# Sums of the gated unit's products stored once in fp32 and split where they are used, with a new set of order constraints, in a two-layer encoder kernel

## The chip, the cores and the metric

The kernel runs on one core of a Trainium2 chip. The metric is the time of one execution on the device, in microseconds (us). The core has a matrix engine (PE, with its weight load PEld shown apart), a vector engine (DVE), a scalar engine (ACT), a general engine (POOL) and a queue engine (SP) that issues most of the DMA transfers. Each engine runs its own instructions in order.

## The reference, cut to what matters

The program is a two-layer trunk over 1024 frames of width 1024, in fp32, with batch 1. The part that the change touches is layer 0:

```python
proj = h @ w_in                      # h = rmsnorm(x); u_s5, g_s5, q, k, v, g_ret
y = gelu(s5(u_s5))                   # diagonal state-space layer
y = y * sigmoid(y @ glu_w + glu_b)   # the gated unit ("GLU")
y_s5 = y * silu(g_s5)
y_ret = retention(q, k, v) * silu(g_ret)     # 8 heads, normalised per head
x = x + concat([y_s5, y_ret]) @ w_out
```

Layer 1 is a convolution module (two pointwise products, a depthwise convolution of width 31, a layer norm, swish, a gate and an output product). A final norm ends the program.

## The kernel before

Activations are held transposed: 128 features on the partitions, time along the row, in two halves of 512 columns. Every fp32 product is made as three matmuls on numbers split into a high and a low part (`mm3`): high weight by high operand (L300), high weight by low operand (L301), low weight by high operand (L302). A matmul of 128x512 is the unit of the work of PE. For weights and operands alike ACT makes the high part (a cast, L278 for weights, L1489 for operands) and DVE or POOL subtracts it from the fp32 original to get the low part (L279 for weights, L1491 for operands).

The program runs in stages: input products and state-space layer (to about 316 us); keys, queries, values and retention, in four pairs of heads numbered 0 to 3 (to about 537 us); the products of the gated unit (`mm_glu...`, to about 610 us); the output product of layer 0 (`mm_wo`); and layer 1.

The product of the gated unit is done by a Strassen-like scheme: seven products of half size instead of eight, on sums of the four quarters of y and of the weights. `y_pass` makes the sums of y: for each of four row blocks (0 to 3) it loads two blocks of state-space output, applies gelu, stores the result to `yn_d` and forms the sums (`yn`, on POOL for the late passes, L1177 to L1180). For each of its two tiles it then casts to a high part `th` on ACT (L1184), stores that from ACT's queue (L1185), subtracts it on DVE (L1186, in place) and stores the low part from SP's queue (L1187). `glu_sums` does the like for the weights on POOL (`gs`, L1200 to L1203, stored to `ws_d`).

`layer0_back_and_layer1` runs the products. Its operands are `y11`, `y21`, `y22` (quarters, loaded in fp32 by `load_split` and split on the chip) and `yt1` to `yt4` (sums, loaded by `load_sum` as two ready halves, high and low, L1531). Product numbers are in the tile names: `mm_glu10` is product 1, `mm_glu60` product 6 and so on. `wf_glu0` to `wf_glu13` are its weight tiles as loaded, `wh_glu` and `wl_glu` the halves; each has three buffers. `gated` applies tanh, multiplies by `yg` and `yn` and splits the result to `ysh` and `ysl`.

Within a pair of retention, PE transposes the keys (`ktp`), DVE scales them (`kt`, L1388), PE makes states (`kv`) and scores (`sp`), DVE masks the scores (`sc`, L1428) and accumulates states (`S`), PE makes the outputs (`ro`), DVE takes their statistics (`st`, `mv`), ACT normalises (`on`, L1471, three buffers), PE transposes back (`rt`, L1479) and DVE multiplies by the gate (`grl`). Queries and keys are rotated before that by POOL (`krot`, `qrot`, L1282), after a transfer swaps their rows (`kswp`, `qswp`).

What sets the order: a scheduler orders each engine's instructions from a timeline of its own, and the table `ORDER` adds constraints. An entry (engine, late, early) says that on that engine the instruction named `late` is placed after the one named `early`; it sets places in a queue, and no engine waits for another by it. SP issues transfers strictly in its order, and an issue waits there until its source is written and its destination buffer is free.

Of the kernel before, what the change touches and what calls it, by code (L numbers as in the profile page):

```python
# [39 lines left out]
LANES = 2  # L40
ADDS = {"k": lambda nc: nc.gpsimd, "q": lambda nc: nc.gpsimd}
ORDER = (
    ('PE', ('turn', 0), ('mm_u6_0', 23)),
    ('PE', ('mm_u6_1', 0), ('turn', 3)),
    ('PE', ('v0_0', 0), ('mm_g8_0', 23)),
    ('PE', ('v1_0', 0), ('mm_g8_0', 23)),
    ('PE', ('kp_0', 0), ('mm_g8_0', 23)),
# [41 lines left out]
    ('PE', ('mm_wo0_0', 42), ('mm_wo1_0', 8)),  # L89
# [64 lines left out]
class Trunk:  # L154
# [995 lines left out]
    def y_pass(self, k, yp=None, tag="ynt"):  # L1150


        nc, v = self.nc, self.nc.vector
        held = yp is None
        pools = [self.rq, self.rq if held else yp]
        yns, yts = [], []
# [23 lines left out]
        eng.tensor_tensor(b21, b11, b21, op=ALU.subtract)  # L1180
        yield
        for i in range(2):
            hi = pools[i].tile([P, T], F32R, name=f"th{i}_{k}", tag="yp", bufs=1)
            nc.scalar.copy(hi[:], yns[i])  # L1184
            nc.scalar.dma_start(self.t_d[i, 0, k * P:(k + 1) * P], hi[:].bitcast(F32))  # L1185
            v.tensor_tensor(yns[i].bitcast(F32R), yns[i], hi[:].bitcast(F32), op=ALU.subtract)  # L1186
# [306 lines left out]
    def layer0_back_and_layer1(self, st):  # L1493
# [665 lines left out]
```

## Time and profile before

| | |
|---|---|
| Time, median of 3 runs | 1134.23 us (1133.91 to 1138.55) |
| Time of the profiled execution | 1135.55 us |
| Its span | 1133.7 us |
| Its mean granted clock of PE | 0.994 |
| PE busy | 1105.6 us (98%) |
| DVE busy | 812.3 us (72%) |
| ACT busy | 543.2 us (48%) |
| POOL busy | 657.0 us (58%) |
| Bytes moved by DMA | 279.47 MB, 247 GB/s on the mean |

The page gives busy time per engine, the span in slices, the DMA queues, the chain of work that ended last, and the costliest groups of instructions. A row of the timeline shows the start, the duration, the engine, the line and operation, out<-in, the shape, and in brackets the idle time of that engine just before, with what released it. A row of the waits shows which engine and line waited for which, the total in us, how often, and the longest. A row of the windows shows for one stretch the busy time of each engine, the granted clock of PE, the share of time in which the DMA engines were busy, and the rate.

### The profile page before, as it was taken

Reading aid. Unit: us, or ns where it says so; the run is one execution under the profiler, and the core shown is the slowest. Engines: PE = TensorE matmul, PEld = TensorE weight load, DVE = VectorE, ACT = ScalarE, POOL = GpSimd, SP = SyncE. Lnnn points to the kernel's source line nnn. Section 1 sums busy time; section 2 is a strip of 40 time slices with the busy share of each in tenths; the row PEclk is TensorE's granted clock in tenths of the full one; section 3 lists DMA queues with packets and bytes.
Section 4 is the critical chain, followed back from the end, with each engine's and each line's share of the span. In section 5 each row is a group of like instructions: output and inputs, shape, how many; then the busy total and the mean of one; then the engine's idle time right before and its main releaser. Section 6 shows DMA issues by size and latency. Waiting matters only on the chain.

```text
span 1133.7 us, 16979 instructions
## 1 busy us (share of the span) xinstructions
PE 1105.6 (98%) x6014; PEld 963.9 (85%) x6014; DVE 812.3 (72%) x1436; ACT 543.2 (48%) x835; POOL 657.0 (58%) x459
## 2 busy tenths in 40 slices
PE   9999999999999999996899999999999999999997
PEld 8888888888888888885778888888888888888886
DVE  6886866666525574578468632599999899999744
ACT  7313334443236541623546523555535677446773
POOL 3049957888455435564375011589544568779863
PEclk9999999999999999998999999999999999999999
DMA  8346767777897767879998998665778665356964
GB/s 318 112 138 172 220 195 239 252 264 263 299 319 240 249 220 260 267 243 289 389 361 290 345 321 272 208 231 198 242 255 291 242 198 177 121 185 233 329 237 176
DMA packets 136117, 279.47 MB, mean 247 GB/s; under 512 B 21089, under 2 KB 50017, under 8 KB 135905
## 3 DMA queue, kind: packets, MB, share of 16 engines
q1 hardware_dynamic: 129744, 257.16, 68.1%
q10 hardware_dynamic: 6288, 21.24, 4.8%
q8 instruction: 47, 0.77, 0.3%
q14 instruction: 38, 0.30, 0.1%
HBM read 191.65 MB, written 82.51 MB: 242 GB/s over the span
## 4 chain that ended last, share of the span: by engine, by line
PE 85%; DMA 5%; DVE 3%; ACT 2%; POOL 2%; issue 2%; SPq 0%; POOLq 0%; DVEq 0%; ACTq 0%
PE mm_g L300 7%; PE mm_g L302 7%; PE mm_g L301 7%; PE mm_v L1374 5%; PE mm_wo L302 5%; PE mm_wo L300 5%; PE mm_wo L301 5%; PE mm_b L301 2%; PE mm_b L302 2%; PE mm_a L301 2%; PE mm_b L300 2%; PE mm_a L302 2%; PE mm_a L300 2%; PE mm_u L301 2%; PE mm_u L300 2%; PE mm_u L302 2%
## 5 line engine op out<-in xcount | busy, mean ns | idle before, releaser
L1776 DVE SCALAR_TENSOR_TENSOR cv<-u,convw,cv 128x512 f32<-128x512 f32 x390 | 268.0, 752 | 5.9 <-ACT cv L1743 3.9
L1737 POOL TENSOR_TENSOR tp<-tp,tp 128x512 f32<-128x512 f32 x64 | 82.4, 1288 | 33.0 <-ACT tp L1736 32.1
L300 PE MATMUL mm_g<-xh,wh_g 128*128 128x512 f32 x256 | 97.8, 382 | 0.0
L301 PE MATMUL mm_g<-xl,wh_g 128*128 128x512 f32 x256 | 97.1, 379 | 0.0
L302 PE MATMUL mm_g<-xh,wl_g 128*128 128x512 f32 x256 | 96.0, 379 | 0.0
L567 POOL TENSOR_TENSOR s1q<-s1q,s1q 128x512 f32<-128x512 f32 x12 | 16.7, 1391 | 80.0 <-ACT s1q L562 71.3
L1736 ACT ACTIVATE tp<-u,convw 128x512 f32<-128x512 f32 x64 | 45.3, 718 | 33.4 <-POOL tp L1737 32.6
L300 PEld LDWEIGHTS mm_g<-xh,wh_g 128*128 128x128 f32 x256 | 48.5, 189 | 6.8 <-issue 0.2
L302 PEld LDWEIGHTS mm_g<-xh,wl_g 128*128 128x128 f32 x256 | 48.5, 189 | 6.8
L301 PEld LDWEIGHTS mm_g<-xl,wh_g 128*128 128x128 f32 x256 | 48.5, 189 | 6.6
L301 PE MATMUL mm_oc<-zl,wh_woc 128*128 128x512 f32 (+1 forms) x144 | 51.4, 357 | 0.2 <-DVE zl L1491 0.2
L300 PE MATMUL mm_oc<-zh,wh_woc 128*128 128x512 f32 (+1 forms) x144 | 51.1, 364 | 0.0
L302 PE MATMUL mm_oc<-zh,wl_woc 128*128 128x512 f32 (+1 forms) x144 | 50.8, 356 | 0.0
L300 PE MATMUL mm_g<-h1h,wh_cg 128*128 128x512 f32 x128 | 49.0, 383 | 0.0
L300 PE MATMUL mm_wo<-ysh,wh_wos 128*128 128x512 f32 x128 | 49.0, 382 | 0.0
L302 PE MATMUL mm_wo<-ysh,wl_wos 128*128 128x512 f32 x128 | 48.7, 380 | 0.3 <-DVE wl_wos L279 0.3
L302 PE MATMUL mm_b<-h1h,wl_cb 128*128 128x512 f32 x128 | 48.6, 380 | 0.0
L302 PE MATMUL mm_a<-h1h,wl_ca 128*128 128x512 f32 x128 | 48.6, 379 | 0.0
L301 PE MATMUL mm_g<-h1l,wh_cg 128*128 128x512 f32 x128 | 48.6, 379 | 0.0
L301 PE MATMUL mm_a<-h1l,wh_ca 128*128 128x512 f32 x128 | 48.6, 379 | 0.0
L302 PE MATMUL mm_g<-h1h,wl_cg 128*128 128x512 f32 x128 | 48.6, 379 | 0.0
L301 PE MATMUL mm_wo<-ysl,wh_wos 128*128 128x512 f32 x128 | 48.6, 379 | 0.0
(650 smaller groups left out, 3505.4 us busy)
## 6 DMA issues: line engine op xcount, KB each, us to landing
wf_g<-w_ab SPq DMA_DIRECT2D x16, 512.0 KB
wf_wos<-w_out SPq DMA_DIRECT2D x16, 512.0 KB
wf_wor<-w_out SPq DMA_DIRECT2D x16, 512.0 KB
wf_cb<-w_c SPq DMA_DIRECT2D x16, 512.0 KB
wf_ca<-w_c SPq DMA_DIRECT2D x16, 512.0 KB
wf_woc<-w_out_c SPq DMA_DIRECT2D x16, 512.0 KB
wf_cg<-w_c SPq DMA_DIRECT2D x11, 512.0 KB
x<-xT SPq DMA_DIRECT2D x8, 512.0 KB
```

What stands on the lines that cost most here:

```text
L300: nc.tensor.matmul(ps, wh[:, kb, :], xh, start=start, stop=False, **more)
L301: nc.tensor.matmul(ps, wh[:, kb, :], xl, start=False, stop=False, **more)
L302: self.last_mm = nc.tensor.matmul(ps, wl[:, kb, :], xh, start=False, stop=stop, **more)
L567: nc.gpsimd.tensor_tensor(a, a, sq[:], op=ALU.add)
L1374: nc.tensor.matmul(us[b][:], l[:, o], r, start=fresh and k == n == 0, stop=k == 3 and n == 2, **({} if fresh else {"skip_group_check": True}))
L1736: nc.scalar.mul(sk[:], u[:, k:k + HALF], cw[:, nb, k:k + 1])
L1737: gp.tensor_tensor(s0[:], s0[:], sk[:], op=ALU.add)
L1776: v.scalar_tensor_tensor(dst[:], *tap, accs_[i][:], op0=ALU.mult, op1=ALU.add)
```

## The change

1. `t_d` keeps one fp32 copy of each sum instead of a high and a low half. `y_pass` no longer casts, no longer stores from ACT's queue and no longer subtracts; the store from SP's queue stays and holds the fp32 sum.
2. `load_sum` loads that copy by `load_split` with `wide=False`: each of 16 tiles of 128x512 comes by one transfer instead of two, into a buffer tagged `tp` (three of these), is cast by ACT and subtracted by DVE.
3. `ORDER` gets 47 entries and loses seven.

```diff
 ORDER = (
+    ('PE', ('ro1_2', 0), ('mm_q2_1', 23)),
+    ('PE', ('rt0_1', 0), ('mm_q1_1', 23)),
+    ('PE', ('mm_glu10', 1), ('ktp0_3', 3)),
+    ('DVE', ('grl_4', 1), ('kt_3', 0)),
+    ('PE', ('mm_glu11', 0), ('rt0_5', 3)),
+    ('PE', ('mm_glu10', 4), ('kv0_3', 7)),
...
+    ('DVE', ('y21l0', 0), ('sc1_3', 1)),
+    ('Pool', ('gs0_3', 0), ('qrot_3', 1)),
+    ('Pool', ('gs1_3', 0), ('qrot_3', 1)),
+    ('Pool', ('yn_3', 0), ('qrot_2', 1)),
...
-    ('SP', ('yt2h0', 0), ('qswp_3', 3)),
+    ('SP', ('yt2f0', 0), ('qswp_3', 3)),
-    ('Activation', ('th0_0', 0), ('mm_v3', 0)),
-    ('SP', ('yr_d', 0), ('qswp_1', 3)),
-    ('Activation', ('th0_3', 0), ('on_5_1', 3)),
...
-        self.t_d = dt("t_d", [2, 2, HALF, T])
+        self.t_d = dt("t_d", [2, HALF, T])
...
         for i in range(2):
-            hi = pools[i].tile([P, T], F32R, name=f"th{i}_{k}", tag="yp", bufs=1)
-            nc.scalar.copy(hi[:], yns[i])
-            nc.scalar.dma_start(self.t_d[i, 0, k * P:(k + 1) * P], hi[:].bitcast(F32))
-            v.tensor_tensor(yns[i].bitcast(F32R), yns[i], hi[:].bitcast(F32), op=ALU.subtract)
-            self.late.append((2, lambda i=i: nc.sync.dma_start(self.t_d[i, 1, k * P:(k + 1) * P], yns[i])))
+            self.late.append((2, lambda i=i: nc.sync.dma_start(self.t_d[i, k * P:(k + 1) * P], yns[i])))
...
-        def load_sum(name, i, c, h):
-
-            res = []
-            for k in range(4):
-                ops = [self.op_tile(self.opA, f"A{h}", f"{name}{q}{k}") for q in "hl"]
-                for j, o in enumerate(ops):
-                    nc.sync.dma_start(o[:].bitcast(F32), self.t_d[i, j, rows(k), hs(c)])
-                res.append(ops)
-            return res
+        def load_sum(name, i, c, h, behind=None):
+
+            return load_split([self.t_d[i, rows(k), hs(c)] for k in range(4)], name, h, False, behind)
```

The lines that follow show where instructions now stand. Line numbers in the changed kernel are 36 higher for retention (L1479 is L1515 there) and 40 higher for the matmuls (L300 is L340). The first place is PE at the last pair of retention, from the last product of pair 2 to the first scores of pair 3. Before, both products of the first weight tile (24 matmuls, of which the last row is the first below) stood ahead of the transposes:

```order
L302 MATMUL mm_glu11_5514<-y11h3_5479,wl_glu0_5093 128x512
L1479 MATMUL rt0_5_5063<-ident_69,on_5_0_5000 128x128 x4
L1479 MATMUL rt0_4_5069<-ident_69,on_4_0_4980 128x128 x4
L1479 MATMUL rt1_5_5075<-ident_69,on_5_1_5058 128x128 x4
L1479 MATMUL rt1_4_5081<-ident_69,on_4_1_5038 128x128 x4
L1386 MATMUL ktp0_3_5236<-ident_69,krot_3_5103 128x128 x4
L1386 MATMUL ktp1_3_5242<-ident_69,krot_3_5103 128x128 x4
L1405 MATMUL kv0_3_5253<-v_00_3507,kt_3_5235 64x128 x8
L1405 MATMUL kv1_3_5266<-v_01_3508,kt_3_5235 64x128 x6
```

Now, with one matmul of `mm_glu10` and the twelve of `mm_glu11` between the transposes:

```order
L340 MATMUL mm_glu10_5481<-y11h0_5431,wh_glu0_5060 128x512
L1515 MATMUL rt0_5_5031<-ident_69,on_5_0_4968 128x128 x4
L1515 MATMUL rt0_4_5037<-ident_69,on_4_0_4948 128x128 x4
L340 MATMUL mm_glu11_5482<-y11h0_5431,wh_glu0_5060 128x512
...
L342 MATMUL mm_glu11_5482<-y11h3_5447,wl_glu0_5061 128x512
L1515 MATMUL rt1_5_5043<-ident_69,on_5_1_5026 128x128 x4
L1515 MATMUL rt1_4_5049<-ident_69,on_4_1_5006 128x128 x4
L1422 MATMUL ktp0_3_5204<-ident_69,krot_3_5071 128x128 x4
L1422 MATMUL ktp1_3_5210<-ident_69,krot_3_5071 128x128 x4
L341 MATMUL mm_glu10_5481<-y11l0_5432,wh_glu0_5060 128x512
...
L340 MATMUL mm_glu10_5481<-y11h1_5436,wh_glu0_5060 128x512
L1441 MATMUL kv0_3_5221<-v_00_3507,kt_3_5203 64x128 x8
```

The transposes `rt0_5` and `rt0_4` moved ahead of all but one matmul of the gated unit, and the last eleven of `mm_glu10` moved behind `ktp1_3`, around the states `kv`.

The second place is DVE in the same stretch, from the scaled keys of pair 3 to its masked scores. `y21l` is the low part of an operand of the gated unit. Before:

```order
L1388 TENSOR_TENSOR kt_3_5235<-ktp1_3_5242,kdec_3348 128x512
L1491 TENSOR_TENSOR y21l0_5486<-y21f0_5483,y21h0_5485 128x512
L1491 TENSOR_TENSOR y21l1_5491<-y21f0_5483,y21h1_5490 128x512
L1491 TENSOR_TENSOR y21l2_5497<-y21f2_5494,y21h2_5496 128x512
L1491 TENSOR_TENSOR y21l3_5502<-y21f2_5494,y21h3_5501 128x512
L1186 TENSOR_TENSOR yn_7_4866<-yn_7_4866,th1_3_4878 128x1024
L1413 COPY S_3_5252<-kv0_3_5253 128x128
L1428 TENSOR_TENSOR sc0_3_5276<-sp00_3_5278,retmask_3_5089 128x512
L1428 TENSOR_TENSOR sc1_3_5277<-sp01_3_5279,retmask_3_5089 128x512
L1415 SCALAR_TENSOR_TENSOR S_3_5252<-S_3_5252,g128_3346,kv0_3_5253 128x128 x3
L1428 TENSOR_TENSOR sc0_3_5276<-sp10_3_5290,retmask_3_5089 128x512
```

Now:

```order
L1424 TENSOR_TENSOR kt_3_5203<-ktp1_3_5210,kdec_3348 128x512
L1449 COPY S_3_5220<-kv0_3_5221 128x128
L1451 SCALAR_TENSOR_TENSOR S_3_5220<-S_3_5220,g128_3346,kv0_3_5221 128x128 x3
L1451 SCALAR_TENSOR_TENSOR S_3_5220<-S_3_5220,g128_3346,kv1_3_5234 128x128 x3
L1464 TENSOR_TENSOR sc0_3_5244<-sp00_3_5246,retmask_3_5057 128x512
L1464 TENSOR_TENSOR sc1_3_5245<-sp01_3_5247,retmask_3_5057 128x512
L1464 TENSOR_TENSOR sc0_3_5244<-sp10_3_5258,retmask_3_5057 128x512
L1464 TENSOR_TENSOR sc1_3_5245<-sp11_3_5259,retmask_3_5057 128x512
L1527 TENSOR_TENSOR y21l0_5454<-y21f0_5451,y21h0_5453 128x512
L1527 TENSOR_TENSOR y21l1_5459<-y21f0_5451,y21h1_5458 128x512
```

The states and masked scores moved ahead of the four subtractions `y21l`, and the subtractions from `yn` are gone.

The third place is POOL before the weight tile `wl_glu2`. `gs` are sums of weights, `yn` sums of y for the last row block. Before:

```order
L1178 TENSOR_TENSOR yn_3_4860<-yn_3_4860 128x512
L1203 TENSOR_TENSOR gs0_2_4841<-gs0_2_4841 128x512
L1179 TENSOR_TENSOR yn_3_4860<-yn_7_4866,yn_3_4860 128x512
L1180 TENSOR_TENSOR yn_7_4866<-yn_3_4860,yn_7_4866 128x512
L279 TENSOR_TENSOR wl_glu1_5166<-wf_glu1_5164,wh_glu1_5165 128x1024
L1282 TENSOR_TENSOR krot_3_5103<-krot_3_5103,kswp_3_5102 128x512 x2
L1200 TENSOR_TENSOR gs1_3_4850<-gs1_3_4850 128x512
L1201 TENSOR_TENSOR gs1_3_4850<-gs0_3_4849,gs1_3_4850 128x512
L1282 TENSOR_TENSOR qrot_3_5174<-qrot_3_5174,qswp_3_5173 128x512 x2
L1202 TENSOR_TENSOR gs0_3_4849<-gs1_3_4850,gs0_3_4849 128x512
L1203 TENSOR_TENSOR gs0_3_4849<-gs0_3_4849 128x512
L279 TENSOR_TENSOR wl_glu2_5517<-wf_glu2_5515,wh_glu2_5516 128x1024
```

Now:

```order
L1318 TENSOR_TENSOR krot_3_5071<-krot_3_5071,kswp_3_5070 128x512 x2
L1318 TENSOR_TENSOR qrot_3_5142<-qrot_3_5142,qswp_3_5141 128x512 x2
L1236 TENSOR_TENSOR gs1_3_4826<-gs1_3_4826 128x512
L1237 TENSOR_TENSOR gs1_3_4826<-gs0_3_4825,gs1_3_4826 128x512
L1238 TENSOR_TENSOR gs0_3_4825<-gs1_3_4826,gs0_3_4825 128x512
L1239 TENSOR_TENSOR gs0_3_4825<-gs0_3_4825 128x512
L1217 TENSOR_TENSOR yn_7_4842<-yn_7_4842,yn_3_4836 128x512
L1218 TENSOR_TENSOR yn_3_4836<-yn_3_4836 128x512
L1219 TENSOR_TENSOR yn_3_4836<-yn_7_4842,yn_3_4836 128x512
L1220 TENSOR_TENSOR yn_7_4842<-yn_3_4836,yn_7_4842 128x512
L319 TENSOR_TENSOR wl_glu2_5485<-wf_glu2_5483,wh_glu2_5484 128x1024
```

`qrot_3` moved ahead of the sums of weights, and the four sums of y (which stood ahead of `krot_3`) moved behind both.

More of the change, by code (lines that the diff above doesn't have):

```diff
@@ L42 @@
 ORDER = (
+    ('Activation', ('yt2h3', 0), ('gu2_2', 0)),
+    ('Pool', ('co4_0', 1), ('tp6_1_0', 2)),
+    ('PE', ('mm_k0_0', 23), ('mm_k0_1', 22)),
+    ('Activation', ('yn_0', 0), ('wh_vb', 0)),
+    ('Activation', ('yn_0', 1), ('wh_vb', 0)),
+    ('PE', ('ro1_2', 0), ('mm_q2_1', 23)),
+    ('PE', ('rt0_1', 0), ('mm_q1_1', 23)),
+    ('Activation', ('s2q7_0', 0), ('zh2_1', 0)),
+    ('PE', ('mm_glu10', 1), ('ktp0_3', 3)),
+    ('DVE', ('mv_3_0', 2), ('qrot_2', 1)),
+    ('DVE', ('grl_4', 1), ('kt_3', 0)),
+    ('DVE', ('ut_1', 1), ('s5t4', 3)),
+    ('Activation', ('zh3_0', 0), ('sgg4_0', 0)),
+    ('Pool', ('wl_cg7_0', 0), ('csr_1', 0)),
+    ('Activation', ('yt2h2', 0), ('sg0_0', 0)),
+    ('DVE', ('grl_2', 1), ('qrot_2', 1)),
+    ('DVE', ('ysl2_0', 0), ('gu2_2', 0)),
+    ('SP', ('x1l0_1', 0), ('wl_woc2_1', 0)),
+    ('DVE', ('ut_0', 0), ('s5t4', 1)),
+    ('Activation', ('r0_1_dg1', 0), ('r0_1_dg1', 3)),
+    ('DVE', ('yr0l3', 0), ('mm_glu52', 0)),
+    ('DVE', ('cv7_0', 0), ('cv6_0', 23)),
+    ('Pool', ('wl_q0', 0), ('ropek', 2)),
+    ('SP', ('gs_d', 11), ('wl_cg2_1', 0)),
+    ('Pool', ('cq_1', 2), ('wl_woc1_0', 0)),
+    ('SP', ('yp_6', 0), ('qswp_1', 1)),
+    ('SP', ('gl7_0', 0), ('wl_cg2_1', 0)),
+    ('Activation', ('wh_glu4', 0), ('sg1_0', 0)),
+    ('SP', ('gl4_1', 0), ('wl_cg2_1', 0)),
+    ('Pool', ('yg4_0', 0), ('wl_glu7', 0)),
+    ('SP', ('qswp_1', 1), ('qswp_1', 0)),
+    ('PE', ('mm_glu11', 0), ('rt0_5', 3)),
+    ('DVE', ('wl_u5', 0), ('ut_2', 0)),
+    ('Pool', ('cq_1', 3), ('wl_woc1_0', 0)),
+    ('DVE', ('ysl1_0', 0), ('gu3_0', 0)),
+    ('Activation', ('cq_1', 0), ('sgg6_0', 0)),
+    ('Pool', ('wl_cg6_0', 0), ('tp6_1_0', 0)),
+    ('Activation', ('yt2h0', 0), ('gu2_1', 0)),
+    ('Activation', ('yn_d', 7), ('on_5_1', 3)),
+    ('PE', ('mm_glu10', 4), ('kv0_3', 7)),
+    ('SP', ('qswp_1', 0), ('qswp_1', 3)),
+    ('Pool', ('zl4_0', 0), ('csr_1', 0)),
     ('PE', ('turn', 0), ('mm_u6_0', 23)),
-    ('PE', ('mm_u6_1', 0), ('turn', 3)),
     ('PE', ('v0_0', 0), ('mm_g8_0', 23)),
@@ L76 @@
     ('PE', ('ro0_4', 0), ('mm_q3_1', 23)),
-    ('Activation', ('th0_3', 0), ('on_5_1', 3)),
     ('PE', ('mm_oc2_1_0', 2), ('mm_oc0_1_0', 6)),
     ('DVE', ('mm_gluy3', 1), ('mm_gluz0', 0)),
-    ('Pool', ('cs2_1', 0), ('te7_1_0', 1)),
     ('Pool', ('s2q0_0', 1), ('cq_1', 5)),
@@ L88 @@
     ('Pool', ('yg5_1', 0), ('wl_glu12', 0)),
-    ('PE', ('mm_wo0_0', 42), ('mm_wo1_0', 8)),
     ('Activation', ('y22h3', 0), ('mm_gluy0', 0)),
```

## The prediction

> **What bounds the kernel now.** I read the page first, then the chain of waits, then the waits of PE, then windows of 20 us where PE is not full, then the timeline of the engines there.
>
> ```profile
> span 1133.7 us, 16979 instructions
> PE 1105.6 (98%) x6014; PEld 963.9 (85%) x6014; DVE 812.3 (72%) x1436; ACT 543.2 (48%) x835; POOL 657.0 (58%) x459
> PE 85%; DMA 5%; DVE 3%; ACT 2%; POOL 2%; issue 2%; SPq 0%; POOLq 0%; DVEq 0%; ACTq 0%
> ```
>
> PE is the bound: 1133.7 - 1105.6 = 28.1 us is all that it stands idle, and the third row puts 85% of the chain on it. The change leaves PE's number of matmuls as it is, so it can win only idle time of PE, and time in which PE runs below its full clock. Where that lies, windows show (columns: PE, PEld, DVE, ACT, POOL busy us with counts, granted clock, DMA share, GB/s):
>
> ```profile
> 500.00:520.00 20.00, 17.04 (x132) 14.94 (x132) 12.69 (x52) 8.21 (x22) 9.53 (x7) 1.00 0.92 266
> 520.00:540.00 20.00, 12.98 (x121) 11.44 (x118) 18.95 (x48) 7.03 (x16) 9.52 (x6) 0.83 0.85 297
> 540.00:560.00 20.00, 16.41 (x83) 13.86 (x83) 6.39 (x15) 11.35 (x21) 8.96 (x5) 1.00 1.04 396
> 560.00:580.00 20.00, 18.21 (x75) 14.58 (x74) 10.38 (x12) 7.60 (x11) 10.58 (x6) 0.91 1.04 395
> 580.00:600.00 20.00, 20.00 (x95) 17.51 (x94) 17.17 (x20) 9.23 (x14) 15.68 (x9) 1.00 0.92 323
> 960.00:980.00 20.00, 20.00 (x94) 17.55 (x93) 20.00 (x32) 9.50 (x15) 14.17 (x9) 1.00 0.32 107
> 1120.00:1134.00 14.00, 6.56 (x47) 5.60 (x46) 5.98 (x18) 3.01 (x8) 3.75 (x5) 0.84 0.45 150
> ```
>
> In 500 to 600 PE is busy 84.6 us, so 15.4 of its 28.1 idle us lie there: the last pair of retention and the front of the gated unit, which is where the sums T are written and used. Another 7.4 us is the end (last row). The row of 960 shows PE full, with DVE full beside it in the convolution; I come back to it. The waits say what PE lacked:
>
> ```profile
> PE sp L1422 <- DVE sc L1428: 4.7, 1, 4.7
> PE mm_glu L302 <- POOL wl_glu L279: 4.1, 3, 3.2
> PE sp L1422 <- POOL qrot L1282: 2.6, 3, 1.2
> PE rt L1479 <- ACT on L1471: 2.6, 2, 1.4
> PE kv L1405 <- DVE kt L1388: 1.8, 1, 1.8
> PE mm_glu L300 <- ACT wh_glu L278: 1.7, 2, 1.6
> PE mm_v L1374 <- DVE v L1342: 1.0, 1, 1.0
> ```
>
> Together 18.5 us.
>
> **Term 1, the last pair of retention.** The largest wait has its cause in DVE's queue:
>
> ```profile
> 516.85 1.22 DVE L1186 TENSOR_TENSOR yn<-yn,th 128x1024 fp32r<-128x1024 f32 x1
> 519.78 6.35 DVE L1491 TENSOR_TENSOR y21l<-y21f,y21h 128x512 fp32r<-128x512 f32 x4
> 526.05 2.28 DVE L1186 TENSOR_TENSOR yn<-yn,th 128x1024 fp32r<-128x1024 f32 x1
> 528.45 1.27 DVE L1428 TENSOR_TENSOR sc<-sp,retmask 128x512 f32<-128x512 f32 x2
> 529.18 1.86 PE L1422 MATMUL sp<-qrot,krot 64*128 64x128 f32 x13 [4.74 <-DVE sc L1428]
> 515.55 1.09 PE L1479 MATMUL rt<-ident,on 128*128 128x128 f32 x8 [1.16 <-ACT on L1471]
> 522.28 1.16 PE L1422 MATMUL sp<-qrot,krot 64*128 64x128 f32 x16 [1.21 <-POOL qrot L1282]
> 523.96 0.49 PE L1422 MATMUL sp<-qrot,krot 64*128 64x128 f32 x2 [0.51 <-POOL qrot L1282]
> ```
>
> PE's second half of the scores waited for a bank that the masking `sc` had to empty, and `sc` stood behind 6.35 us of `y21l` and 2.28 us of the subtraction that the change removes. In the new order `sc` and the states stand ahead of `y21l`, so all 4.74 us should go. The wait for `kt` (1.80) had the other removed subtraction (1.22) ahead of it, and eleven matmuls of the gated unit now fill PE around it; I leave 0.3 of it. The two waits for `qrot` (1.21 + 0.51) came because POOL did the weights' sums first:
>
> ```profile
> 517.14 2.05 POOL L1200 TENSOR_TENSOR gs<-gs 128x512 f32<-128x512 f32 x1 [10.31 <-DMA yt2l<-t_d]
> 520.51 3.40 POOL L1282 TENSOR_TENSOR qrot<-qrot,qswp 128x512 f32<-128x512 f32 x2
> 507.33 2.97 SPq L1278 DMA_DIRECT2D qswp<-qraw  x4
> 506.93 2.88 ACT L1471 ACTIVATE on<-ro,off,rs 128x128 f32<-128x128 f32 x8
> 506.35 1.98 PE ro L1454 x16
> ```
>
> POOL stood idle 10.31 us at `gs` and ran `qrot` behind it. The swap had been issued by 510.3, so `qrot` directly behind `krot` should be ready near 516, and PE asks for it at about 519: both waits go. The wait for `on` (1.16) goes for `rt1`, which now has twelve matmuls ahead of it.
>
> What is late next is `rt0_5`, now behind a single matmul of the gated unit. PE's last output of pair 2 ends at 506.35 + 1.98 = 508.3, ACT's normalised halves at 506.93 + 2.88 = 509.8. That is a new wait of about 1.5 us; bounds are 0 (ACT keeps pace, since what precedes also moves) and 2.9 (with another of the 1.4 us waits for `on`). I take 1.5.
>
> Removed 4.74 + 1.80 + 1.72 + 1.16 = 9.4, kept or new 0.3 + 1.5 + 0.2 = 2.0. **-7.4 us** (bounds -9.4 and -4.5).
>
> **Term 2, the clock.** The window 520 to 540 shows a granted clock of 0.83 over 12.98 us of busy PE, 560 to 580 shows 0.91 over 18.21. At full clock that is 0.17 x 12.98 = 2.2 and 0.09 x 18.21 = 1.6 us less. The first lies with the 4.74 us wait and goes with it; of the second I take half. **-3.0 us** (bounds 0 and -3.8).
>
> **Term 3, the front: values, keys and first pairs.** From the waits: `mm_v` 1.0; of `qrot` 2.6 - 1.7 = 0.9; of `on` 2.6 - 1.2 = 1.4. The new order puts matmuls of the values ahead of `mm_q0`, and states, outputs and transposes of pairs 0 to 2 behind more of the next projections. Each such matmul of 128x512 covers 20 / 94 = 0.21 us by the 960 to 980 row, so ten or so cover any of these waits. **-3.3 us** (bounds -3.3 and 0).
>
> **Term 4, the gated unit: what T costs and gives.** Removed, from the tiles' own rows:
>
> ```profile
> L1184 ACT CAST th<-yn x8: 1040/1046/1056, 358.9 to 524.7; 128x1024 fp32r<-128x1024 f32 x8
> L1186 DVE TENSOR_TENSOR yn<-yn,th x8: 1215/1224/2279, 360.0 to 526.1; 128x1024 fp32r<-128x1024 f32 x8
> L1185 ACTq DMA_DIRECT2D t_d<-th x8: 326/326/327, 360.0 to 525.7; - x8
> ```
>
> Eight casts (8.4 us of ACT), eight subtractions (about 11 of DVE, two of them, 3.5 us, after 500), eight stores of 512 KB, and half of the 32 loads of 256 KB. Except for those two subtractions this lies beside full PE and is worth nothing itself. Added are sixteen casts on ACT and sixteen subtractions on DVE in the gated unit:
>
> ```profile
> L1489 ACT CAST y21h<-y21f 128x512 fp32r<-128x512 f32 x4 | 2.3, 622 | 3.5 <-DMA yt2h<-t_d 3.5
> 581.40 2.85 DVE L1491 TENSOR_TENSOR y22l<-y22f,y22h 128x512 fp32r<-128x512 f32 x2
> 584.78 1.17 DVE L1491 TENSOR_TENSOR y22l<-y22f,y22h 128x512 fp32r<-128x512 f32 x1
> 592.84 2.46 DVE y22l L1491
> 563.53 6.91 DMA wf_glu<-ws_d
> 550.85 1.26 POOL L1558 TENSOR_TENSOR yg<-yg,yn 128x512 f32<-128x512 f32 x1 [12.47 <-PE mm_glu L302]
> 552.07 7.45 POOL L279 TENSOR_TENSOR wl_glu<-wf_glu,wh_glu 128x1024 fp32r<-128x1024 f32 x3
> ```
>
> ACT has room: 16 x 0.62 = 10 us where it is busy 44 of 100. DVE is the question. It is busy 65.6 us of 500 to 600 now, 62.1 without the two subtractions from `yn`; the same work must fit in about 83 us if PE wins what I say. A split there costs 1.17 to 2.46 us by these rows, 6.35 / 4 = 1.59 for `y21l`. Sixteen at 1.59 are 25.4, in all 87.5 us against 83: DVE nearly full for the whole stretch, so a bound from there too.
>
> The gain is on DMA. In 540 to 580 its share is 1.04 at 395 GB/s, the weight `wf_glu` took 6.91 us, and PE's 4.1 + 1.7 us for `wl_glu` and `wh_glu` come from it. Sixteen loads fewer are 4.19 MB, 10.6 us of transfers at 395 GB/s. Against it stands a coupling: the loads of T now go through three buffers, so SP waits for a split before the fourth, and the weights queue behind it. POOL's four late sums of y stand ahead of `wl_glu2`, and SP's two stores of them ahead of the first `yt2` and `wf_glu3`. I take 60% of the 5.8 us: **-3.5 us** (bounds -5.8 and +4.5, DVE's excess of 87.5 over 83).
>
> The Trainium skill, "SBUF — State Buffer", section "Who interferes with whom", speaks against these sixteen splits: a DVE instruction with two SBUF inputs contends with a POOL instruction that reads SBUF, and whoever starts later blocks for the other's whole length. The trace agrees in direction: `y21l` beside POOL takes 1.59 each, `sc`, with one input from PSUM, 0.64. At its worst, by the rule, each split waits for a whole tile of weights, and the sum would be that of rival S below.
>
> **Sum.** -7.4 - 3.0 - 3.3 - 3.5 = -17.2. From the profiled execution's 1135.55 that gives 1118.4; its own time lies 1.3 above the median of the runs, so by the median 1117. I say **1118**. From 600 on I cost the change at nothing: the same matmuls follow, PE is full, and the convolution's DVE work starts with its inputs, so it shifts with them. If that did not hold, DVE, full in 960 to 980, would make PE wait there and take back up to the whole 17 us.
>
> **Rivals.**
>
> - *F, all goes.* All 15.4 idle us, both clock terms (3.8) and the front (3.3): 22.5, 1113. For it: every cause named above is moved. Against: it needs no new wait at `rt0_5`. Chance 0.15, with some at 1109 if the end gains too.
> - *C, the coupling.* Weights stand behind loads that wait for splits; PE waits at `wl_glu3`, `wl_glu4` or `yt3` as long as it does now (term 4 nothing, or +3), and the second clock loss stays. -7.4 - 2.2 - 3.3 + 3 = -9.9: 1125. For it: 12.47 us lie between POOL's instructions there now, and SP's order is strict. Against: 4 MB less to move. Chance 0.22.
> - *N, no change.* The gains at the pair are handed to waits in the gated unit: PE reaches it 11 us earlier, while DMA, at share 1.04, delivers the weights at the old time. 1130 to 1138. Against: 10.6 us of transfers are gone. Chance 0.10.
> - *S, slower.* One mechanism, in 500 to 600: each split is held by one of POOL's `wl_glu` (7.45 / 3 = 2.48 us), and DVE becomes the bound. A split at 0.64 + 2.48 = 3.12 makes 62.1 + 49.9 = 112 us against 100 now: +12, less 3.3 at the front, 1144. It decides from (100 - 62.1) / 16 = 2.37 us per split on; below 1.31 it costs nothing. For it: one row of 2.46. Against: the mean of the eight splits quoted is (6.35 + 2.85 + 1.17 + 2.46) / 8 = 1.6. Chance 0.07.
>
> The Trainium skill's rule on that page gives S if each split meets a weight tile; the rows bear that out for one split of the eight.
>
> **How the numbers follow.** Forecast 0.46, F 0.15, C 0.22, N 0.10, S 0.07. The forecast's own range is 1113 to 1123, F reaches to 1109, C to 1129; I set 1109 to 1132, which leaves out part of N and S. A measurement of this kernel tells 0.5% from no change, so faster is below 1128.6. Forecast, F and most of C are faster: 0.82; N and the rest of C the same: 0.11; S slower: 0.07.
>
> **What would show it.** Right: `sp` no longer waits for `sc`; `rt` shows one wait of 1 to 2 us behind `mm_glu10`; the clock is 1.00 in the window of the last pair; PE's busy time stays within some us of 1105 and its idle falls to 10 to 14 us; DVE is 80 to 95% busy in the gated unit, with splits near 1.5 us. Wrong: `mm_glu` waits for a `yt` split, `wl_glu` or `wh_glu` for over 6 us in sum (C, N); splits above 2.4 us with DVE at 100% (S); PE idle in the convolution, which no term here has.

## The result, and the profile after

The changed kernel takes 1124.39 us (median of 4 runs, 1122.26 to 1125.38) against 1134.43 us before (median of 4). The ratio is 0.9901, with a 95% interval of 0.9874 to 0.9928: about 10 us faster. The forecast was 1118 us in a range of 1109 to 1132, and faster with a chance of 0.82: direction and range held, the gain is 10 of the 16 us forecast. The measured time lies just above the forecast's own range of 1113 to 1123. The profiled execution of the changed kernel took 1122.26 us, the shortest of its four runs.

Its page first (span, busy time of each engine, the chain that ended last):

```profile
span 1120.5 us, 16970 instructions
PE 1103.2 (98%) x6014; PEld 960.6 (86%) x6014; DVE 818.1 (73%) x1444; ACT 543.5 (49%) x843; POOL 653.8 (58%) x459
PE 89%; DMA 4%; DVE 2%; POOL 1%; issue 1%; ACT 1%; SPq 0%; POOLq 0%; DVEq 0%; ACTq 0%
```

PE's idle time fell from 28.1 us to 1120.5 - 1103.2 = 17.3, and its busy time by 2.4 with the same 6014 matmuls. PE's share of the chain that ended last rose from 85 to 89%. DVE is busy 5.8 us more. The windows of the stretch that the prediction was about (the columns are those of the prediction's windows):

```profile
500.00:520.00 20.00, 18.68 (x176) 16.31 (x176) 14.62 (x58) 9.32 (x25) 10.71 (x9) 1.00 0.68 216
520.00:540.00 20.00, 16.06 (x91) 13.04 (x90) 15.16 (x50) 11.13 (x25) 7.31 (x5) 0.94 1.00 378
540.00:560.00 20.00, 20.00 (x95) 17.21 (x94) 15.42 (x16) 12.87 (x23) 13.54 (x7) 0.98 0.94 334
560.00:580.00 20.00, 19.54 (x88) 15.93 (x86) 18.32 (x19) 9.36 (x15) 19.22 (x9) 1.00 0.90 295
580.00:600.00 20.00, 18.32 (x83) 15.25 (x82) 17.84 (x26) 15.23 (x25) 15.08 (x9) 1.00 0.95 316
```

PE is now busy 92.6 us of 500 to 600 where it was 84.6. The window of 520 still lacks 3.9 us, and the clock there is 0.94 where it was 0.83. The windows are not the same places of the program any more, since everything from about 500 on comes earlier, but the missing time can be read. DVE went from 65.6 to 81.4 us in these hundred: it stays the second fullest engine, and is now at 81%. The DMA share in 540 to 580 fell from 1.04 to 0.94 and 0.90. What PE waits for now:

```profile
PE rt L1515 <- ACT on L1507: 3.0, 2, 1.7
PE mm_glu L340 <- ACT wh_glu L318: 1.9, 2, 1.0
PE mm_glu L340 <- ACT sg L1596: 1.3, 1, 1.3
PE rf_R L675 <- DVE rf_dg L672: 1.0, 2, 0.8
PE mm_v L1410 <- ACT v L1360: 0.7, 1, 0.7
PE mm_glu L342 <- POOL wl_glu L319: 0.5, 1, 0.5
PE mm_glu L340 <- DVE gu L1643: 0.4, 1, 0.4
```

The waits of `sp` for `sc` (4.7) and `qrot` (2.6) and of `kv` for `kt` (1.8) are gone, and the one for `wl_glu` fell from 4.1 to 0.5. Two lines weigh most now, both on ACT: `rt` still waits for `on` (3.0, before 2.6, but at other places), and a product waits for `sg`, which is new. The timeline of ACT shows why (idle before, in brackets):

```profile
530.74 0.62 ACT L1525 CAST yt2h<-yt2f 128x512 fp32r<-128x512 f32 x1 [2.78 <-DMA yt2f<-t_d]
531.26 1.50 ACT L1507 ACTIVATE on<-ro,off,rs 128x128 f32<-128x128 f32 x4
535.07 1.28 ACT L1596 ACT_TABLE_LOAD   x1
```

And that of PE, with the two transposes that waited:

```profile
534.74 1.09 PE L1515 MATMUL rt<-ident,on 128*128 128x128 f32 x8 [1.71 <-ACT on L1507]
506.04 1.09 PE L1515 MATMUL rt<-ident,on 128*128 128x128 f32 x8 [1.32 <-ACT on L1507]
```

The second row is the wait that the prediction gave as new, 1.5 us at `rt0_5`: 1.32. The first row is `rt0_7`, which it did not have. ACT stood idle 2.78 us at `yt2h0`, one of the casts that the change adds, because the transfer of its sum had not landed; the normalisation `on_6_0` stood behind it, and `sg` behind the normalisations and a table load.

### The profile page after: what moved, and what is told of

It reads as the page before. It is cut to its first block, busy times and chain, and to the rows that moved or that the text cites. A ratio compares the mean times of both kernels' runs of the same rounds, so it can differ in the third digit from the quotient of the medians.

```text
span 1120.5 us, 16970 instructions
## 1 busy us (share of the span) xinstructions
PE 1103.2 (98%) x6014; PEld 960.6 (86%) x6014; DVE 818.1 (73%) x1444; ACT 543.5 (49%) x843; POOL 653.8 (58%) x459
## 4 chain that ended last, share of the span: by engine, by line
PE 89%; DMA 4%; DVE 2%; POOL 1%; issue 1%; ACT 1%; SPq 0%; POOLq 0%; DVEq 0%; ACTq 0%
PE mm_g L340 7%; PE mm_g L341 7%; PE mm_g L342 7%; PE mm_wo L341 5%; PE mm_wo L340 5%; PE mm_wo L342 5%; PE mm_v L1410 5%; PE mm_a L340 2%; PE mm_b L341 2%; PE mm_a L341 2%; PE mm_b L342 2%; PE mm_a L342 2%; PE mm_b L340 2%; PE mm_oc L341 2%; PE mm_oc L340 2%; PE mm_oc L342 2%
## 5 line engine op out<-in xcount | busy, mean ns | idle before, releaser
L340 PE MATMUL mm_g<-xh,wh_g 128*128 128x512 f32 x256 | 97.7, 382 | 0.0
L607 POOL TENSOR_TENSOR s1q<-s1q,s1q 128x512 f32<-128x512 f32 x12 | 17.2, 1433 | 80.7 <-ACT s1q L602 80.7
L340 PEld LDWEIGHTS mm_g<-xh,wh_g 128*128 128x128 f32 x256 | 48.4, 189 | 6.8 <-issue 0.2
L340 PE MATMUL mm_oc<-zh,wh_woc 128*128 128x512 f32 (+1 forms) x144 | 50.7, 363 | 0.0
L340 PE MATMUL mm_g<-h1h,wh_cg 128*128 128x512 f32 x128 | 48.9, 382 | 0.0
L340 PE MATMUL mm_wo<-ysh,wh_wos 128*128 128x512 f32 x128 | 48.9, 382 | 0.0
L340 PE MATMUL mm_a<-h1h,wh_ca 128*128 128x512 f32 x128 | 48.6, 380 | 0.0
L340 PE MATMUL mm_b<-h1h,wh_cb 128*128 128x512 f32 x128 | 48.5, 379 | 0.0
L341 PE MATMUL mm_b<-h1l,wh_cb 128*128 128x512 f32 x128 | 48.5, 379 | 0.0
```

The costliest lines, as they stand in the source:

```text
L340: nc.tensor.matmul(ps, wh[:, kb, :], xh, start=start, stop=False, **more)
L341: nc.tensor.matmul(ps, wh[:, kb, :], xl, start=False, stop=False, **more)
L607: nc.gpsimd.tensor_tensor(a, a, sq[:], op=ALU.add)
```

## The experiments

The changed kernel was run once more beside three others as their base.

> The changed kernel itself, run once more, as the base of the three kernels beside it on the same chip. Its earlier runs had a median of 1124.4 us (1122.3 to 1125.4). Expected 1123 to 1125, with the same waits: `rt` for `on` twice (3.0 us), `mm_glu` for `wh_glu` (1.9) and for `sg` (1.3).

Measured: 1124.37 us (median of 4), ratio to before 0.9904 (0.9884 to 0.9923). The waits for `on` (3.1) and `sg` (1.3) are the same. `mm_v` waits 2.1 us for `v` and not 0.7, `wh_glu` makes PE wait 0.7 and not 1.9, and `mm_gluy` 0.8 and not 0.2. The two profiled executions differ by 2.1 us; PE's idle time in them differs by 0.7 and its busy time by 1.3, so no single wait explains it. The granted clock dips in the window of 540 (0.91) and not in that of 520 (1.00).

**The data alone.**

```diff
 # the changed kernel with the table ORDER of the kernel before, and in it
-    ('SP', ('yt2h0', 0), ('qswp_3', 3)),
+    ('SP', ('yt2f0', 0), ('qswp_3', 3)),
-    ('Activation', ('th0_0', 0), ('mm_v3', 0)),
-    ('Activation', ('th0_3', 0), ('on_5_1', 3)),
```

> The change of the data alone: sums T stored in fp32 and split on the chip, with the order constraints of the kernel before (the two that name the removed casts `th` left out, the one on `yt2h0` now naming the load `yt2f0`). Theory A (the order at the last pair and at the front makes most of the gain): 1128 to 1133 us; PE still waits for `sc`, 2 to 4 us, since `y21l` stands ahead of it. Rival B (the removed subtractions, stores and loads make most of it): 1121 to 1126.

Measured: 1141.58 us (median of 6), ratio 1.0058 (1.0034 to 1.0082). Both theories had it faster than before; it is 7 us slower. PE's waits:

```profile
PE mm_glu L298 <- ACT y21h L1483: 8.0, 1, 8.0
PE sp L1416 <- POOL qrot L1276: 4.9, 2, 4.5
```

The timeline of its ACT and its SP queue:

```profile
534.44 0.62 ACT L1483 CAST yt2h<-yt2f 128x512 fp32r<-128x512 f32 x1 [13.04 <-DMA yt2f<-t_d]
534.96 0.61 ACT L1483 CAST y21h<-y21f 128x512 fp32r<-128x512 f32 x1
522.92 6.53 SPq L1199 DMA_DIRECT2D ws_d<-gs  x2
```

The cast of `yt2` came early in ACT's queue, its load was issued late (SP stood at the store of `ws_d` until 529.5), and ACT waited 13 us for it with the cast of `y21` behind, which PE needed. In the kernel before, `yt2` was loaded ready and had no cast; the longest wait of ACT put down to one of its transfers is 3.46 us. The second wait, 4.5 us for `qrot`, lies at an earlier pair of heads: SP issued a load of `y_pass` (`yp`, at 432.7) ahead of the swap `qswp`, whose issue ended at 436.9, where it had ended at 432.9 in the kernel before.

**The order alone.**

```diff
 # the kernel before with the table ORDER of the changed kernel, and in it
-    ('Activation', ('yt2h3', 0), ('gu2_2', 0)),
-    ('Activation', ('yt2h2', 0), ('sg0_0', 0)),
-    ('Activation', ('yt2h0', 0), ('gu2_1', 0)),
-    ('SP', ('yt2f0', 0), ('qswp_3', 3)),
+    ('SP', ('yt2h0', 0), ('qswp_3', 3)),
```

> The order constraints of the changed kernel on the data of the kernel before: T is stored and loaded as two halves, made by `th` and the subtraction from `yn` (the three constraints that name casts of `yt2` are left out, the one on the load of `yt2` names its high half). Theory A: 1124 to 1129 us; `sp` does not wait for `sc` any more; the gated unit keeps waits for weights of 4 to 8 us, since DMA moves 4 MB more there. Rival B: 1130 to 1135.

Measured: 1132.58 us (median of 10), ratio 0.9970 (0.9953 to 0.9987): 2 us. The time lies in rival B's range and not in theory A's. The wait for `sc` that theory A saw gone is larger than before (6.0 us, at `ro` in place of `sp`), and the waits for weights are 3.1 us where it gave 4 to 8. PE's waits:

```profile
PE ro L1486 <- DVE sc L1465: 6.0, 1, 6.0
PE rt L1516 <- ACT on L1508: 5.4, 2, 4.1
```

The timeline of its DVE and ACT:

```profile
531.08 1.23 DVE L1223 TENSOR_TENSOR yn<-yn,th 128x1024 fp32r<-128x1024 f32 x1 [5.45 <-POOL yn L1217]
532.48 1.28 DVE L1465 TENSOR_TENSOR sc<-sp,retmask 128x512 f32<-128x512 f32 x2
529.73 1.04 ACT L1221 CAST th<-yn 128x1024 fp32r<-128x1024 f32 x1 [10.42 <-POOL yn L1216]
```

The new order puts POOL's sums of y behind `qrot` and the sums of weights. With the old data a cast on ACT and a subtraction on DVE wait for these sums; both stand in queues that PE needs, and `sc` is behind. The same stands at an earlier pair, in the rows of DVE and PE there:

```profile
457.46 1.22 DVE L1223 TENSOR_TENSOR yn<-yn,th 128x1024 fp32r<-128x1024 f32 x1 [10.54 <-POOL yn L1217]
471.11 1.97 PE L1516 MATMUL rt<-ident,on 128*128 128x128 f32 x8 [4.10 <-ACT on L1508]
```

The window of 460 to 480 has a granted clock of 0.83 there, and 1.00 in the changed kernel. At the transposes `rt0_5` both kernels have run 3110 matmuls, the changed one at 506.04 us and this one at 515.34. After 3290 matmuls, about the end of the last pair, it is 18.0 us behind, and at the end 11.5. It loses about as much ahead of the last pair as in it, and makes up some 6 us behind it, where its sums T come loaded ready. So with this order the gain at the pairs needs the removal of `th`, and the new data need the order. Alone they make +7 and -2 us, together -10.

**The same, with the subtraction moved.** One constraint more on top of that kernel:

```diff
+    ('DVE', ('yn_3', 0), ('sc1_3', 1)),
```

> The kernel of order_only (new constraints, old data) with one more constraint on DVE: the subtraction from `yn_3` stands behind the masked scores. In order_only DVE stood idle 5.45 us at that subtraction, waiting for POOL's sums of y, which the new order puts behind the weights' sums, and `sc` and PE's outputs waited behind it (6.0 us). If that is why the new order alone gains only 2 us: the wait for `sc` falls under 1 us and the time from 1132.6 to 1126 to 1129. If the old data hold it up elsewhere too (weights in the gated unit, DMA), over 1130.

Measured: 1139.81 us (median of 6, 1136.93 to 1146.40), ratio 1.0059 (1.0028 to 1.0090). The wait of 6.0 us for `sc` at this pair is gone, as expected (1.3 us for `sc` remain in the whole program), but the time is 7 us longer. Its profiled execution was the slowest of the six, 6.6 us above the median. PE's waits:

```profile
PE mm_glu L337 <- ACT wh_glu L315: 10.8, 2, 8.9
PE mm_glu L339 <- POOL wl_glu L316: 5.1, 3, 2.6
```

The timeline of its ACT:

```profile
535.98 1.04 ACT L1221 CAST th<-yn 128x1024 fp32r<-128x1024 f32 x1 [11.47 <-POOL yn L1216]
541.72 1.04 ACT L1221 CAST th<-yn 128x1024 fp32r<-128x1024 f32 x1 [2.63 <-DMA t_d<-th]
544.54 1.03 ACT L315 CAST wh_glu<-wf_glu 128x1024 fp32r<-128x1024 f32 x1
```

At this pair ACT's half of the same chain now holds the path: `th` waits 11.47 us for POOL's sums, the second `th` for the store of the first, and the weight's cast `wh_glu` comes only at 544.5. The scheduler also moved ten matmuls of `mm_glu12`, which need that weight, further ahead on PE. So the constraint moved the wait from DVE to ACT. That does not explain the 7 us: both kernels have run 3276 matmuls when PE waits for this `wh_glu`, at 545.6 us here and at 542.5 in the kernel without the constraint, and they were 3.6 us apart at `rt0_5` already. The other 9.5 us between the two profiled executions arise behind it, where the granted clock is 0.74 in the window of 540 to 560 and the waits for `wl_glu` are 5.1 us against 1.3. In the changed kernel, which has no `th`, PE waits 0.95 us at this place.

**The order of the last pair.** Eight constraints taken out of the changed kernel, and one of them alone:

```diff
 # both runs
-    ('DVE', ('y21l0', 0), ('sc1_3', 1)),
 # pair3_undone only
-    ('PE', ('mm_glu10', 1), ('ktp0_3', 3)),
-    ('DVE', ('grl_4', 1), ('kt_3', 0)),
-    ('PE', ('mm_glu11', 0), ('rt0_5', 3)),
-    ('PE', ('mm_glu10', 4), ('kv0_3', 7)),
-    ('Pool', ('gs0_3', 0), ('qrot_3', 1)),
-    ('Pool', ('gs1_3', 0), ('qrot_3', 1)),
-    ('Pool', ('yn_3', 0), ('qrot_2', 1)),
```

> The changed kernel without eight constraints that order the last pair (`mm_glu10` behind `ktp0_3` and `kv0_3`, `mm_glu11` behind `rt0_5`, `kt_3` behind `grl_4`, `y21l0` behind `sc1_3`, `gs0_3` and `gs1_3` behind `qrot_3`, `yn_3` behind `qrot_2`). Term 1 of the prediction: the waits of the last pair (`rt`, `kv`, `sp`) come back by 5 to 8 us in the windows of 500 to 540, time 1128 to 1132. If it is not these constraints that removed them: 1123 to 1126.

> The changed kernel without the one constraint that puts `y21l` behind the masked scores `sc` on DVE. Term 1: the scheduler puts `y21l` ahead of `sc` again, PE waits for `sc` at `sp` by 2 to 5 us, and the time rises by as much over the changed kernel, though `rt0_7` may then wait less. If the removed subtraction from `yn` was what mattered, the wait stays under 1 us and the time does not move by more than 1.

Measured: 1130.22 us without the eight (ratio 0.9942, 0.9922 to 0.9962) and 1129.73 without the one (0.9942, 0.9925 to 0.9959), against 1124.4 with them: 5.8 and 5.4 us longer. The first time is inside the expectation of term 1. The waits at `sp` and `kv` came back by 5.7 us, but those at `rt` fell from 3.0 to 1.2, so the sum of the three is 3.9 where 5 to 8 were expected. PE's longest wait without the eight:

```profile
PE sp L1450 <- DVE sc L1456: 5.0, 1, 5.0
```

And without the one:

```profile
PE sp L1457 <- DVE S L1450: 3.8, 1, 3.8
```

And DVE's row ahead of it:

```profile
515.09 5.13 DVE L1526 TENSOR_TENSOR y21l<-y21f,y21h 128x512 fp32r<-128x512 f32 x3
```

`y21l` stands ahead again, and the wait is of the size expected, though the trace puts it down to `S`, which stands between `y21l` and `sc`. In both runs the granted clock of the window 520 to 540 is 0.83 again, as in the kernel before; the changed kernel has 0.94 and its second run 1.00. The 5.4 us are not this wait alone: `rt0_7` and `sg` no longer make PE wait, and waits in the gated unit (`wl_glu` 2.5, `mm_gluy` 2.2, `gu` 1.8) have grown. Once this constraint is out, the other seven change the time by 0.5 us, less than the runs' spread; what they are worth with it in place was not run.

**The cast that holds ACT.**

```diff
+    ('Activation', ('yt2h0', 0), ('on_7_0', 3)),
```

> The changed kernel with one more constraint of order on ACT: the cast `yt2h0` stands behind `on_7_0`. In the changed kernel ACT stood idle 2.78 us at `yt2h0`, whose transfer had not landed, and the normalisation `on_6_0` queued behind it; then PE waited 1.71 us at `rt0_7` for `on` and 1.27 us for `sg`. Theory A (the added casts hold what queues behind them on ACT): the wait at `rt0_7` falls under 0.5 us, the one for `sg` under 0.8, time 2 to 3 us below the run of the changed kernel beside it. Rival B (DVE takes the statistics too late, behind `y21l`): the wait at `rt0_7` stays over 1.2 us and the time does not move by more than 1.

Measured: 1125.59 us (median of 5, 1121.43 to 1130.72), ratio 0.9930 (0.9905 to 0.9955), which cannot be told from the changed kernel. PE's waits in its profiled execution, which was its shortest:

```profile
PE mm_glu L340 <- DVE gu L1643: 4.2, 2, 2.8
PE mm_glu L340 <- ACT wh_glu L318: 1.5, 1, 1.5
PE rt L1515 <- ACT on L1507: 1.3, 1, 1.3
PE mm_glu L340 <- ACT sg L1596: 0.3, 1, 0.3
```

The timeline of its DVE:

```profile
550.11 0.69 DVE L1527 TENSOR_TENSOR yt3l<-yt3f,yt3h 128x512 fp32r<-128x512 f32 x1 [1.10 <-ACT yt3h L1525]
552.08 0.68 DVE L1643 TENSOR_TENSOR gu<-gu,mm_glu 128x512 f32<-128x512 f32 x1
```

The mechanism of theory A is shown: the wait at `rt0_7` is gone and PE waits 0.3 us for `sg`. Its price is not: the scheduler also shifted DVE's order, and PE waits 4.2 us for `gu`, a sum on DVE behind subtractions of T that wait for their own casts. One of these casts, of `yt3`, stood 2.99 us on ACT for its transfer. The 3 us were handed on to DVE.

**Three edits that tried to keep that gain.** Each adds to the changed kernel:

```diff
 # on_and_weight_first
+    ('Activation', ('yt2h0', 0), ('on_7_0', 3)),
+    ('Activation', ('rs_7_0', 0), ('wh_glu2', 0)),
+    ('Activation', ('gu2_0', 0), ('wh_glu2', 0)),
 # splits_last_on_DVE
+    ('Activation', ('yt2h0', 0), ('on_7_0', 3)),
+    ('DVE', ('yt3l2', 0), ('gu2_0', 0)),
+    ('DVE', ('yt1l1', 0), ('gu3_2', 0)),
 # quarter_on_POOL
+    ('Activation', ('yt2h0', 0), ('on_7_0', 3)),
-                self.split(f, a, b, v, behind)
+                self.split(f, a, b, nc.gpsimd if name in ("yt1", "yt3") and i % 2 else v, behind)
```

> The changed kernel with two more constraints on ACT: `rs_7_0` and `gu2_0` stand behind the weight's cast `wh_glu2`. With these the scheduler also puts `on_6_0` and `on_7_0` ahead of the casts of `yt2` behind the first. In the changed kernel `wh_glu2` stood behind `rs_6_0`, which waited for DVE's statistics, though its tile had been loaded long before, and PE waited 0.95 us. Theory A: that wait goes too, 3 to 4 us below the changed kernel beside it. Rival B: under 1.5 us, since the statistics stay where they are.

> The kernel of cast_behind_on with two more constraints on DVE: `yt3l2` behind the sum `gu2_0`, `yt1l1` behind the sum `gu3_2`. In cast_behind_on PE waited 4.2 us for `gu`, which stood on DVE behind subtractions of T whose transfers had not landed. Theory: in an in-order queue a split with a late transfer must stand behind what PE waits for; the waits for `gu` fall by 2 to 3.5 us and the time to 1119 to 1122. If DVE is simply full, the waits move to another of its products (`mm_gluy`, `mm_gluz`) and the time stays at 1124 to 1126.

> The kernel of cast_behind_on with four of the sixteen subtractions of T (`yt3l1`, `yt3l3`, `yt1l1`, `yt1l3`) on POOL. DVE loses about 6 us of work, POOL gains 4 x 1.3 = 5 in a stretch where it is busy 55 of 80 us and also makes `wl_glu`. If DVE is the bound: waits for `gu` and `mm_gluy` fall by 2 to 4 us, time 1120 to 1123. If POOL's own order then delays `wl_glu`: waits for `wl_glu` over 2 us, time 1124 or more.

Measured: 1127.51 us (ratio 0.9934, 0.9912 to 0.9956), 1129.72 (0.9951, 0.9935 to 0.9968) and 1130.30 (0.9959, 0.9942 to 0.9976). All three are slower than the changed kernel; the first expectation had a gain in both of its cases. In the first, which also holds the constraint of `cast_behind_on`, the wait at `rt0_7` is gone; `wh_glu2` did not move ahead of `rs_6_0`; instead `gu2_0` moved behind both, and two matmuls that need the weight moved ahead on PE, which waited for it (and 3.2 us for `gu`):

```profile
PE mm_glu L340 <- ACT wh_glu L318: 3.5, 1, 3.5
```

In the second the waits for `gu` fell from 4.2 to 2.1 us, but others took their place:

```profile
PE mm_glu L340 <- ACT wh_glu L318: 2.6, 2, 1.5
PE mm_glu L340 <- DVE gu L1643: 2.1, 3, 0.7
PE mm_glu L342 <- POOL wl_glu L319: 1.9, 2, 1.0
PE mm_glu L340 <- DVE mm_gluy L1640: 1.5, 1, 1.5
```

One wait moved to `mm_gluy`, as the expectation gave it for the case "DVE is simply full". More went to the weights on ACT and POOL, and the time is worse than either case gave, so neither is shown. In the third the wait for `gu` is still 3.9 us and the one for `wl_glu` 1.3, so neither of its two cases is shown either; why it is slower stays open.

**What the subtractions cost.** They were made twice, and left out:

```diff
 # splits_twice, behind the split in load_split
+                if name[:2] == "yt":
+                    v.tensor_tensor(b[:], f, a[:].bitcast(F32), op=ALU.subtract)
 # no_low_of_T, the same place
-                self.split(f, a, b, v, behind)
-                res.append((a, b))
+                self.split(f, a, b, v, behind) if name[:2] != "yt" else nc.scalar.copy(a[:], f)
+                res.append((a, a if name[:2] == "yt" else b))
```

> The changed kernel with each of the sixteen subtractions of the sums T on DVE made twice (the second writes the same values again). Rival S of the prediction in its form of a price: if DVE is close to being the bound of the gated unit, the time rises by 5 to 10 us (in 520 to 600 DVE is busy 66.7 of 80 us; sixteen more at about 1.4 make 89). If the splits lie beside other work with room, the time rises by 0 to 2 us.

> The changed kernel without the sixteen subtractions on DVE: the products take the high part of T in place of its low part, so the low part of these sums is left out of the result; number and form of the matmuls, the transfers and the casts stay. It prices what the sixteen subtractions still cost where they stand. If DVE is next to the bound of the gated unit (doubling them cost 13 us): 3 to 6 us below the changed kernel's 1124.4, with the waits of PE for DVE's `gu` and `mm_gluy` gone and the wait at `rt0_7` for `on` still there, since the casts still hold ACT. If the first sixteen were hidden and only the second sixteen were not: 1123 to 1125.

Measured: twice 1137.71 us (median of 10, ratio 1.0027, 1.0011 to 1.0043), 13.3 us above the changed kernel and 3.3 above the kernel before; left out 1120.90 (median of 4, ratio 0.9883, 0.9858 to 0.9909), 3.5 below it, with intervals that overlap (0.9858 to 0.9909, 0.9884 to 0.9923). Two of the groups of DVE in 500 to 620 of the changed kernel (busy us, mean ns of one):

```profile
L1527 DVE TENSOR_TENSOR yt1l<-yt1f,yt1h 128x512 fp32r<-128x512 f32 x4 | 7.4, 1860 | 0.0
L1527 DVE TENSOR_TENSOR yt2l<-yt2f,yt2h 128x512 fp32r<-128x512 f32 x4 | 4.0, 1008 | 5.4 <-ACT yt2h L1525 5.4
```

PE's longest wait in the kernel with twice the subtractions:

```profile
PE mm_glu L340 <- DVE gu L1645: 10.6, 6, 3.6
```

And two of its windows:

```profile
560.00:580.00 20.00, 12.54 (x57) 10.03 (x56) 19.93 (x21) 7.59 (x12) 14.14 (x9) 1.00 0.72 245
580.00:600.00 20.00, 16.02 (x71) 12.84 (x70) 19.97 (x23) 7.48 (x13) 8.83 (x4) 1.00 0.71 240
```

With sixteen more, DVE is full in these windows and PE waits for it. The first sixteen are busy 7.4 + 4.0 and, for `yt3` and `yt4`, 5.8 + 5.4 us, together 22.6, and cost about 3.5; the second sixteen add 838.4 - 821.3 = 17.1 us of DVE by the pages of this run and of the second run of the changed kernel, and cost 13.3. DVE stands close to the point where it decides. Without them PE's waits for `gu` are gone and those on ACT stay (`rt` 2.8, `wh_glu` 2.7, `sg` 1.3), as expected of the casts. But the wait for `gu` was only 0.4 us. Of the 2.8 us between the two profiled executions 0.7 lie in PE's idle time and 2.1 in its busy time, about 1.4 of these by the clock in the windows of 520 and 540. So the 3.5 us are the price of the subtractions as a whole, and most of it is not a wait for DVE; where the rest comes from stays open.

## Why the prediction was right, and where it was short

**Bound and place.** Right. PE's idle time was the stock to win from: 8.0 us of it went in 500 to 600 by the windows. PE's busy time fell by 2.4 us in the profiled execution and by 1.1 in that of the second run. Of the 28.1 us of idle time 17.3 remain, where the forecast's signs had 10 to 14.

**Term 1, the last pair (-7.4; the sum of its waits moved by -5.1).** The cause named for the largest wait is shown by the run without the one constraint, where 3.8 us came back at `sp`, the clock of 0.83 with it, and 5.4 us in the time, part of them in the gated unit. The waits for `kt` and `qrot` went as worked out, and `rt0_5` waits 1.32 for 1.5 forecast. The step that fell short is "what is late next", which stopped at `rt0_5`. It went through PE and DVE and not through ACT's queue: `rt0_7` (1.7 us) and `sg` (1.3 us) wait because an added cast of `yt2` holds ACT for its transfer. The prediction had the coupling of loads and splits only for SP, as rival C, with weights behind loads; what came is of the same kind, at another place. Against 9.4 us before, 1.3 + 1.7 + 1.3 = 4.3 remain.

**Term 2, the clock (-3.0).** 0.06 x 16.06 + 0.02 x 20.00 = 1.4 us are left of 3.8: -2.4. In the second run 0.09 x 20.00 = 1.8 are left: -2.0. That the loss in the last pair's window goes with the wait there is borne out by the two runs without its constraints, which show 0.83 again.

**Term 3, the front (-3.3).** Of its 3.3 us of waits, 0.7 remain in one profiled execution and 2.1 in the other, at `mm_v`: -2.6 and -1.2. The waits at `qrot` and `on` of the earlier pairs are gone in both. Which constraints did it was not tried apart. With the last pair's eight undone the kernel is still 4.5 us faster than before; that is what the rest of the change does without them, in this stage and the others.

**Term 4, the gated unit (-3.5).** From 5.8 us to 1.9 + 0.5 for weights and 0.4 for `gu`: -3.0 (in the second run 0.7 + 0.5 for weights, 0.4 for `gu` and 0.8 for `mm_gluy`: -3.4). The 60% was close. It was a choice, and the cause named, fewer loads, is not shown: no run tries it apart. The largest of these waits before, 3.2 us, ended with the `wl_glu` of 552.07, which stood in POOL's queue behind `yg` (550.85), while its cast had ended by 548.96. In the changed kernel the first `yg` runs at 534.79, ahead of these weights. So the order on POOL may have won it; whether `yg` itself waited for a transfer stays open. The price taken for a split, 1.59 us, was 22.6 / 16 = 1.41. The Trainium skill's rule on DVE and POOL ("SBUF — State Buffer", "Who interferes with whom") has the trace with it in direction: 1.0 to 1.9 us by group where `sc` took 0.68, and within `yt2l` 0.69 us for a split with no POOL instruction beside it and 1.96 for the one beside `wl_glu`. Rival S took each split to wait for a whole tile, 3.12 us; that did not come, the longest of the sixteen took 2.25.

**The sum.** The four terms make -13.1 by the profiled executions, which differ by 13.3, for -17.2 forecast. Term 1 is 2.3 us of that difference. The median of the runs moved by 10.0, less than the two profiled executions, since the profiled run before lay 1.1 us above its median and the one after 2.1 below. The second run's profiled execution (1124.34) lies at the median: there the terms make -5.0 - 2.0 - 1.2 - 3.4 = -11.6, for -11.2 measured, so against the medians terms 1 and 3 fell short by about 2 us each. The removed waits add up to the time only roughly, since each was read by itself.

**The rivals.** S did not happen, but its decision point was near: it put the free point at 1.31 us for each split and the loss of the whole gain at 2.37. At 1.41 the splits cost 3.5 us; doubled, at (22.6 + 17.1) / 16 = 2.48 for each pair, the kernel stands 3.3 us behind the kernel before. C gave 1125, and the measured time is next to that, but by chance: its mechanism, weights that keep PE waiting as long as before, did not come, since their waits fell from 5.8 us to 2.4. What it had on SP, a queue that stands for a transfer, came on ACT. N did not happen, and F did not, with 17.3 us of idle time left.

**What the prediction did not see** is that the two halves of the change are worth little apart. It added the removed work and the new order up in one sum and did not ask what either does alone; the runs show +7 and -2 apart and -10 together.

## What to carry to other kernels

Work that waits for a transfer, put into the in-order queue of an engine, delays all that stands behind it (ACT stood 2.78 us for a cast here, and 13.04 with the data alone); before a load is replaced by a load and a cast, look at what queues behind the cast on that engine and when its transfer lands, on every engine that gets a part. Where a change of data and a change of order come together, price them as one: each can remove what the other would have waited for. And a wait removed from one engine can come back on the next in the chain: with one cast moved, PE's waits went from ACT to DVE, which was close to full here.

## What was not expected

Three edits, each against a wait that the trace showed, made the kernel 3 to 6 us slower. In the first the scheduler moved other instructions with the constraints, and PE waited for those; in the other two new waits are shown and what brought them is not. And cast_behind_on, with one added constraint, spread wider than its base: five runs from 1121.4 to 1130.7 us, the changed kernel from 1122.3 to 1125.5 over eight runs, with the granted clock at 0.994 to 0.999 in the former and 0.995 to 1.000 in the latter. What of the spread is the clock and what the waits was not settled.
